# Dummy products in the first stage and a regrouped start of the output projection, in a one-core hybrid SSD / Gated DeltaNet layer

## The chip, the cores and the metric

The kernel runs on one core of one Trainium2 chip. The metric is device time in microseconds, the median of the runs shown. TensorE (PE) runs the matrix products and loads its weights on a side path (PEld); VectorE (DVE), ScalarE (ACT) and GpSimd (POOL) work beside it, and SyncE (SP) issues nearly all DMA transfers of this kernel.

## What is computed

One layer of a hybrid decoder for two request groups, 1024 prompt tokens and 64 sample tokens (8 requests of 8 tokens), 1088 in all, with the same weights. Cut to what matters:

```python
h = _rms_norm(x, norm_mix_pre) * (1 + sc1) + sh1        # sc1, sh1: from silu(c) @ w_ada + b_ada
proj = h @ w_in                                         # 1024 -> z, xbc, dt, qkv, gate, beta, alpha
...
y = _rms_norm(y_ssd * silu(z), ssd_norm_w)              # 1024 columns, chunked SSD scan
o = _rms_norm(o_gdn, gdn_norm_w) * silu(gate)           # 1024 columns, chunked Gated DeltaNet
mixed = jnp.concatenate([y, o], axis=-1)                # 2048 columns
m = mixed @ w_out
x = x + g1 * _rms_norm(m, norm_mix_post)
h = _rms_norm(x, norm_ffn_pre) * (1 + sc2) + sh2
gu = h @ w_gate_up
x = x + g2 * _rms_norm((silu(gu[..., :D_FF]) * gu[..., D_FF:]) @ w_down, norm_ffn_post)
```

The new states of both mixers, for prompt and samples, are returned too.

## The kernel before

Every float32 product is done as three matmuls of split operands: `hh` by `wh`, `hl` by `wh` and `hh` by `wl`, where `wh` is the rounded value of a weight (a cast on ACT, line 173) and `wl` the rest (a subtraction on DVE, line 174). A half of a weight tile, 128 x 512, is loaded by SP into a buffer `wr` (line 181) of a pool; the pools have few such buffers, so the next load waits until a `wr` has been split.

**Tokens** lie in three groups `TH` of 384, 384 and 320 columns; the last holds the 64 samples. There are KD = 8 blocks of 128 input columns.

**First stage.** The conditioning vector goes through `w_ada`; then the tokens are normalised (`norm_x`), turned by PE (`turned`, line 339, three transposes for a block of a group), and modulated (`modulated`, lines 357 to 368: ACT writes `hh`, DVE writes `ht` and, with POOL, `hl`; the samples' columns are added on lines 363, 365 and 367). As soon as a block is there, `first_k` (lines 416 to 418) multiplies it with the first two tiles of `w_in`: six matmuls for one block. For group 0 this is written out; for groups 1 and 2 `first_group` goes over k, modulating block k and multiplying block k-2. In between the tasks that `tick()` advances put small transposes of convolution states (`halos`, line 391). After this stage jobs take the rest of `w_in` (lines 198 to 200).

**Output projection.** `gemm_rows` is called once for each group, with 16 steps of 128 of the 2048 columns of `mixed`. A step takes a block of `mixed` (loaded by `mixed_load`, line 1331, from `mixdr`), splits it into `sh` (ACT, line 1398) and `sl` (DVE, line 1399), and multiplies with two halves of `w_out`: 18 matmuls (lines 1386, 1388, 1389) of 512 columns. Below, step 0 to step 47 counts over all three groups. In every group the steps take the DeltaNet half of the columns first (k = 8 to 15) and then the SSD half (k = 0 to 7), whose blocks are multiplied on DVE with row factors `RB` (line 1458). Weights of even k go through pool `wp`, which is shared with the work before, those of odd k through pool `wo`, which is new. The mixed blocks of groups 0 and 1 go through pool `mxp` for even k and `g_` for odd k, where `g_` takes memory that the SSD part has left; four blocks are asked for ahead. Group 2's are asked for after all tasks have ended (`settle()`), two ahead.

Beside the steps run tasks that advance with `tick()`, four times in a step: the samples' DeltaNet (`gdn_samples`, lines 1463 to 1620, with loads of `smx`, `s_d`, `s_eg` on lines 1465 to 1475), and the evacuation of a finished group.

**Order.** PE executes in the order of the program. The other engines and SP's queue are put in order by a scheduler that keeps each waiting for its operands in that order, so a load that stands behind another on SP waits for it.

Of the kernel before, what the change touches and what calls it, by code (L numbers as in the profile page):

```python
# [16 lines left out]
P = 128  # L17
# [26 lines left out]
def hybrid_step(ctx: ExitStack, tc: tile.TileContext, x_p, x_s, c_p, c_s, st_ssd, st_ssdc, st_gdn, st_gdnc,  # L44
# [100 lines left out]
    def wait(n):  # L145
        for _ in range(n):
            yield
# [109 lines left out]
    def norm_x(i):  # L257
        n = P if i < NC else NS
        xt = xts[i]
        jk = init.tile([P, D], BF16, name="jk")  # L260
        act.activation(out=jk[0:n], in_=xt[0:n], func=AF.Square, accum_out=ss[0:n, i:i + 1])
        rsqrt_small(rs[0:n, i:i + 1], ss[0:n, i:i + 1], 1.0 / D, EPS)
        dve.tensor_scalar(out=xt[0:n], in0=xt[0:n], scalar1=rs[0:n, i:i + 1], scalar2=None, op0=ALU.mult)
# [69 lines left out]
    def turned(g, k):  # L333

        n = TH[g][1]
        ps = bank()
        for w in range(0, n, P):
            r = min(P, n - w)
            pe.transpose(ps[:, w:w + r], xts[3 * g + w // P][0:r, k * P:(k + 1) * P], ident[0:r, 0:r])
        return ps  # L340
# [31 lines left out]
    def mod(g, k, ps):  # L372
        c0, n = TH[g]
        modulated(ps, k, c0, n, hh[k][:, c0:c0 + n], hl[k][:, c0:c0 + n], init, pool if k % 2 else dve)
# [34 lines left out]
    first, loads = zip(*(tile_halves(c) for c in (C_K, C_Q)))  # L409
    first_ps = [ps_a.tile([P, 512], F32, name="ps")[:, 0:TH[0][1]] for _ in first]  # L410

    def first_k(g, k, pss):
        t0, n = TH[g]
        xh, xl = hh[k][:, t0:t0 + n], hl[k][:, t0:t0 + n]
        for (hi, lo), o in zip(first, pss):
            pe.matmul(o, lhsT=hi[k], rhs=xh, start=(k == 0), stop=False)
            pe.matmul(o, lhsT=hi[k], rhs=xl, start=False, stop=False)
            pe.matmul(o, lhsT=lo[k], rhs=xh, start=False, stop=(k == KD - 1))

    def first_group(g):  # L420

        pss = [ps_a.tile([P, 512], F32, name="ps")[:, 0:TH[g][1]] for _ in first]
        for k in range(KD + 2):
            if k < KD:
                mod(g, k, turned(g, k))
            if k >= 2:
                first_k(g, k - 2, pss)
                tick()
        hid_box[g] = clock[0]
        return pss  # L430
# [36 lines left out]
    with tc.high_priority(-80):  # L467
        for i in range(3, NT):
            norm_x(i)
    for k in range(4, KD):  # L470
        first_k(0, k, first_ps)
    hid_box[0] = clock[0]
# [853 lines left out]
    mxp = ph_b.enter_context(tc.tile_pool(name="mxp", bufs=1, side="right", reuse_waits="tile"))  # L1326
    ahead = []

    def mixed_load(k, c0, n):
        t = (g_ if queue and k % 2 else mxp).tile([P, 384], F32, name="mx", bufs=3)  # L1330
        sp.dma_start(out=t[:, 0:n], in_=mixdr[k * P:(k + 1) * P, c0:c0 + n])
        return t

    settle(ssd_run)
    ph_a.close()

# [7 lines left out]
    GS = [mid.tile([NS, D], F32, name="gs0")]  # L1344
    RB = [mid.tile([P, T], F32, name=f"RB{g}") for g in range(2)]
    late_box = {}
    KS = list(range(KD, 2 * KD)) + list(range(KD))

    queue, last = [(k, *TH[gi]) for gi in range(2) for k in KS], []
    for i in range(4):  # L1350
        ahead.append(mixed_load(*queue.pop(0)))

    def load_gains(i, gp, gs):
        sp.dma_start(out=gp, in_=gaindr[i][0].partition_broadcast(P))
# [95 lines left out]
    def mixed_piece(c0, n):  # L1450
        def piece(k):
            m = ahead.pop(0)
            if queue or last:
                ahead.append(mixed_load(*(queue or last).pop(0)))
            if k < KD:
                while "RB" not in late_box:
                    tick()
                dve.scalar_tensor_tensor(out=m[:, 0:n], in0=m[:, 0:n], scalar=W_SSDN[:, k:k + 1],
                                         in1=RB[k // 4][:, c0:c0 + n], op0=ALU.mult, op1=ALU.mult)
            return m[:, 0:n]  # L1460
        return piece

    def gdn_samples():
        smx = g_.tile([P, HG, 4, NS], F32, name="smx")
        sp.dma_start(out=smx, in_=smdr)
        smp, smv, smg = smx[:, :, 0:2, :], smx[:, :, 2, :], smx[:, :, 3, :]
        ko = g_.tile([NS, HG, P], F32, name="s_ko")
# [5 lines left out]
        sp.dma_start(out=d0, in_=accr[16:24, NP:T].partition_broadcast(NS))  # L1473
        eg = g_.tile([P, HG, NS], F32, name="s_eg")
        sp.dma_start(out=eg, in_=eaccr[16:24, NP:T].partition_broadcast(P))
        yield from wait(16)
        for a in range(2):
            ps = bank()
            pv = ps.rearrange("p (h n) -> p h n", n=P)
# [227 lines left out]
    def second_half():  # L1707
# [5 lines left out]
        yield from wait(8)  # L1713
        yield from flips(GRP[1][1:], t, 2 * HN, 6 * P)

    def w_out_half(k, hf):
        return load_half(w_out[k * P:(k + 1) * P, hf * 512:hf * 512 + 512], wp=wo if k % 2 else wp)

    ph_f = ExitStack()
    for gi, grp in enumerate(GRP):  # L1720
# [19 lines left out]
            xts[i] = hv  # L1740
            return after

        gemm_rows(grp, KS, w_out_half, mixed_piece(c0, n), mid, done)
        if gi == 1:
            settle()
            last += [(k, *TH[2]) for k in KS]
            for i in range(2):
                ahead.append(mixed_load(*last.pop(0)))
            ph_s.close()
            ph_c.close()  # L1750
            acs_ = ctx.enter_context(tc.tile_pool(name="acs", bufs=2, reuse_waits="tile"))
            wf = ctx.enter_context(tc.tile_pool(name="wf", bufs=1, reuse_waits="tile"))
            h2b = ph_f.enter_context(tc.tile_pool(name="h2b", bufs=1, reuse_waits="tile"))
            blocks(h2b, 0)
            x1t = xts
            spawn(later(second_half(), 22))
        elif gi == 0:
            spawn(later(flips(GRP[0], xts, 0, 3 * P), FLIP))
# [214 lines left out]
```

## Time and profile before

| what | value |
|---|---|
| median of 3 runs | 2013.7 us |
| lowest and highest run | 2012.06 and 2014.39 us |
| the profiled execution | 2012.82 us |
| its span in the trace | 2011.0 us |
| PE, busy share of the span | 97% |
| DVE, ACT, POOL busy shares | 67%, 51%, 6% |
| mean granted clock of PE | 0.987 |

A page of the profile gives, for one execution, the busy time of each engine and the chain of work that ended last. Views of the trace answer narrower questions: a table of waits says what an engine sat idle for; a timeline gives single instructions with the idle time before them in brackets and who ended it; a table of windows gives busy time of every engine in a stretch with the granted clock of PE, where 1.00 is 2.4 GHz and 0.50 is 1.2 GHz. Times in a timeline are us from the start of the span. The first 87 us are the first stage; the output projection runs from about 1003 to 1266 us.

### The profile page before, as it was taken

How to read it: one execution, taken by the hardware profiler on the slowest of the kernel's cores; microseconds unless marked ns; L12 is line 12 of the kernel's file. 1: busy time of each engine (PE TensorE's matmuls, PEld its weight loads, DVE VectorE, ACT ScalarE, POOL GpSimd, SP SyncE). 2: the span in 40 equal slices, each digit the busy share in tenths (PEclk: the TensorE clock that was granted, in tenths of full speed). 3: DMA queues.
4: the chain of work that ended last, by engine and by line, in shares of the span. 5: the costliest groups of instructions: out<-in, count | busy, mean ns of one | idle time of the engine just before them, and what ended most of it. 6: DMA issues, size and time to landing. Idle time of an engine off the chain costs nothing.

```text
span 2011.0 us, 35475 instructions
## 1 busy us (share of the span) xinstructions
PE 1951.5 (97%) x13211; PEld 1753.8 (87%) x13211; DVE 1351.1 (67%) x2964; ACT 1035.2 (51%) x2578; POOL 125.9 (6%) x184
## 2 busy tenths in 40 slices
PE   6999999999999999999969999999999999999998
PEld 4898899999999998998857677899999999988886
DVE  4669767877887766867657767885555556645465
ACT  4455455554655446777435666753333334544454
POOL 2100000000000001100011010100000000000000
PEclk9799999999999999999989999999999999999999
DMA  8223323322211127555267855422222224633131
GB/s 300 56 60 102 97 81 110 100 81 87 84 52 55 59 83 189 177 138 159 77 212 228 258 184 192 127 75 81 75 76 82 76 81 128 225 125 110 46 100 50
DMA packets 223142, 235.29 MB, mean 117 GB/s; under 512 B 19018, under 2 KB 177252, under 8 KB 222842
## 3 DMA queue, kind: packets, MB, share of 16 engines
q1 hardware_dynamic: 220266, 228.86, 36.8%
q10 hardware_dynamic: 2384, 3.05, 0.4%
q8 instruction: 104, 1.70, 0.3%
q0 software_dynamic: 320, 1.12, 0.2%
q14 instruction: 68, 0.56, 0.1%
HBM read 188.83 MB, written 44.15 MB: 116 GB/s over the span
## 4 chain that ended last, share of the span: by engine, by line
PE 84%; DVE 6%; ACT 3%; DMA 3%; issue 2%; SPq 1%; POOL 1%; DVEq 0%; POOLq 0%; ACTq 0%
PE ps L198 9%; PE ps L199 8%; PE ps L200 8%; PE ps L1874 7%; PE ps L1873 7%; PE ps L1875 7%; PE ps L1386 7%; PE ps L1389 7%; PE ps L1388 6%; PE ps L741 2%; PE ps L795 1%; DMA wr<-in_w_out_dram 1%; PE ps L704 1%; DVE uc L891 1%; DMA L<-accr 1%
## 5 line engine op out<-in xcount | busy, mean ns | idle before, releaser
L198 PE MATMUL ps<-hh,wh 128*128 128x384 f32 (+1 forms) x1200 | 425.6, 355 | 0.1
L200 PE MATMUL ps<-hh,wl 128*128 128x384 f32 (+1 forms) x1200 | 393.0, 327 | 0.0
L199 PE MATMUL ps<-hl,wh 128*128 128x384 f32 (+1 forms) x1200 | 392.6, 327 | 0.0
L1386 PE MATMUL ps<-wh,sh 128*128 128x512 f32 x678 | 274.6, 405 | 16.0 <-ACT wh L173 15.2
L1389 PE MATMUL ps<-wl,sh 128*128 128x512 f32 x678 | 267.7, 395 | 0.2 <-DVE wl L174 0.2
L198 PEld LDWEIGHTS ps<-hh,wh 128*128 128x128 f32 x1200 | 227.1, 189 | 17.1 <-issue 11.5
L1388 PE MATMUL ps<-wh,sl 128*128 128x512 f32 x604 | 237.6, 393 | 3.7 <-DVE sl L1399 3.7
L199 PEld LDWEIGHTS ps<-hl,wh 128*128 128x128 f32 x1200 | 227.3, 189 | 0.8
L200 PEld LDWEIGHTS ps<-hh,wl 128*128 128x128 f32 x1200 | 226.0, 188 | 0.0
L173 ACT CAST wh<-wr 128x512 fp32r<-128x512 f32 x200 | 122.7, 621 | 171.0 <-PE ps L199 84.5
L174 DVE TENSOR_TENSOR wl<-wr,wh 128x512 fp32r<-128x512 f32 x200 | 136.8, 691 | 58.5 <-ACT wh L173 57.8
L1386 PEld LDWEIGHTS ps<-wh,sh 128*128 128x128 f32 x678 | 128.4, 189 | 52.4 <-ACT wh L173 15.6
L174 DVE TENSOR_TENSOR wl<-wd,wh 128x512 fp32r<-128x512 f32 x130 | 89.6, 692 | 118.1 <-ACT wh L173 114.8
L1389 PEld LDWEIGHTS ps<-wl,sh 128*128 128x128 f32 x678 | 128.4, 189 | 30.3 <-DVE wl L174 0.8
L173 ACT CAST wh<-wd 128x512 fp32r<-128x512 f32 x130 | 80.7, 621 | 139.0 <-PE ps L1388 100.3
L1388 PEld LDWEIGHTS ps<-wh,sl 128*128 128x128 f32 x604 | 114.5, 190 | 27.3 <-DVE sl L1399 4.5
L1810 ACT CAST wh<-s 128x512 fp32r<-128x512 f32 x104 | 64.4, 620 | 83.1 <-PE ps L1874 74.6
L1873 PE MATMUL ps<-T_0h,wh 128*128 128x272 f32 x352 | 102.0, 290 | 3.3 <-DVE u L1889 1.8
L1874 PE MATMUL ps<-T_0l,wh 128*128 128x272 f32 x352 | 101.6, 289 | 0.0
L1874 PE MATMUL ps<-T_1l,wh 128*128 128x272 f32 x352 | 101.6, 289 | 0.0
L1875 PE MATMUL ps<-T_0h,wl 128*128 128x272 f32 x352 | 101.3, 288 | 0.0
L1875 PE MATMUL ps<-T_1h,wl 128*128 128x272 f32 x352 | 101.3, 288 | 0.0
(496 smaller groups left out, 4442.6 us busy)
## 6 DMA issues: line engine op xcount, KB each, us to landing
wr<-in_w_in_dram SPq DMA_DIRECT2D x104, 256.0 KB
wr<-in_w_gate_up_dram SPq DMA_DIRECT2D x104, 256.0 KB
wr<-in_w_out_dram SPq DMA_DIRECT2D x96, 256.0 KB
w<-in_w_ada_dram SPq DMA_DIRECT2D x16, 1024.0 KB
wd<-in_w_down_dram SPq DMA_DIRECT2D x22, 512.0 KB
actdr<-as SPq DMA_DIRECT2D x18, 544.0 KB
L<-accr SPq DMA_DIRECT2D x16, 544.0 KB
am<-actdr SPq DMA_DIRECT2D x44, 192.0 KB
```

What stands on the lines that cost most here:

```text
L173: act.copy(wh, src)
L174: low.tensor_tensor(out=wl, in0=src, in1=wh.bitcast(F32), op=ALU.subtract)
L198: pe.matmul(out, lhsT=hi[k], rhs=xh[k], start=(k == 0), stop=False)
L199: pe.matmul(out, lhsT=hi[k], rhs=xl[k], start=False, stop=False)
L200: pe.matmul(out, lhsT=lo[k], rhs=xh[k], start=False, stop=(k == KD - 1))
L1386: pe.matmul(o, lhsT=sh[:, cs], rhs=wh, start=first, stop=False)
L1388: pe.matmul(o, lhsT=sl[:, cs], rhs=wh, start=False, stop=False)
L1389: pe.matmul(o, lhsT=sh[:, cs], rhs=wl, start=False, stop=last)
L1810: act.copy(wh, opa[p])
L1873: pe.matmul(o, lhsT=wh[:, cs], rhs=bh[:, m, :], start=(m == 0 and not on), stop=False, **on)
L1874: pe.matmul(o, lhsT=wh[:, cs], rhs=bl[:, m, :], start=False, stop=False, **on)
L1875: pe.matmul(o, lhsT=wl[:, cs], rhs=bh[:, m, :], start=False, stop=(m == 3), **on)
```

## The change

It has three parts. First, a function `keep_busy(n)` issues n products of the first modulated block with the first weight block into a bank of PSUM that nobody reads: 14 before group 0's blocks 4 to 7, and 10 each before `first_k(1, 0)` and `first_k(2, 0)`. Second, in the output projection the pools of the weights go by the number of the step: steps 0 and 1 use `wp`, then even steps `wo` and odd steps `wp`. Mixed blocks: the first three in `mxp`, then odd ones of groups 0 and 1 in `g_`, all of group 2 in `mxp`; three are asked for ahead instead of four (two from group 2 on), in one queue over all groups, and group 2 takes its steps in the order k = 0 to 15. Third, `gdn_samples` issues its loads 6 ticks later and everything after them 4 ticks, which is one step, later.

```diff
+    def keep_busy(n):
+
+        ps = bank()
+        for i in range(n):
+            pe.matmul(ps[:, 0:384], lhsT=first[0][0][0], rhs=hh[0][:, 0:384], start=True, stop=True)
+
...
         for k in range(KD + 2):
             if k < KD:
                 mod(g, k, turned(g, k))
+            if k == 2:
+                keep_busy(10)
             if k >= 2:
...
     with tc.high_priority(-80):
         for i in range(3, NT):
             norm_x(i)
+    keep_busy(14)
     for k in range(4, KD):
         first_k(0, k, first_ps)
...
-    def mixed_load(k, c0, n):
-        t = (g_ if queue and k % 2 else mxp).tile([P, 384], F32, name="mx", bufs=3)
-        sp.dma_start(out=t[:, 0:n], in_=mixdr[k * P:(k + 1) * P, c0:c0 + n])
-        return t
...
-    KS = list(range(KD, 2 * KD)) + list(range(KD))
-
-    queue, last = [(k, *TH[gi]) for gi in range(2) for k in KS], []
-    for i in range(4):
-        ahead.append(mixed_load(*queue.pop(0)))
+
+    KS = [list(range(KD, 2 * KD)) + list(range(KD))] * 2 + [list(range(2 * KD))]
+    queue = [(gi, k) for gi in range(3) for k in KS[gi]]
+    asked = [0]
+
+    def mixed_load():
+
+        i = asked[0]
+        asked[0] += 1
+        gi, k = queue[i]
+        c0, n = TH[gi]
+        t = (g_ if gi < 2 and i > 2 and i % 2 else mxp).tile([P, 384], F32, name="mx", bufs=3)
+        sp.dma_start(out=t[:, 0:n], in_=mixdr[k * P:(k + 1) * P, c0:c0 + n])
+        ahead.append(t)
+
+    for i in range(3):
+        mixed_load()
...
             m = ahead.pop(0)
-            if queue or last:
-                ahead.append(mixed_load(*(queue or last).pop(0)))
+            while asked[0] < len(queue) and len(ahead) < (3 if asked[0] < 4 * KD else 2):
+                mixed_load()
...
     def gdn_samples():
         smx = g_.tile([P, HG, 4, NS], F32, name="smx")
+        yield from wait(6)
         sp.dma_start(out=smx, in_=smdr)
...
-        yield from wait(16)
+        yield from wait(14)
...
+    steps = [0]
+
     def w_out_half(k, hf):
-        return load_half(w_out[k * P:(k + 1) * P, hf * 512:hf * 512 + 512], wp=wo if k % 2 else wp)
+        steps[0] += 1
+        return load_half(w_out[k * P:(k + 1) * P, hf * 512:hf * 512 + 512],
+                         wp=wo if steps[0] > 4 and steps[0] % 4 in (1, 2) else wp)
...
-        gemm_rows(grp, KS, w_out_half, mixed_piece(c0, n), mid, done)
+        gemm_rows(grp, KS[gi], w_out_half, mixed_piece(c0, n), mid, done)
         if gi == 1:
             settle()
-            last += [(k, *TH[2]) for k in KS]
-            for i in range(2):
-                ahead.append(mixed_load(*last.pop(0)))
             ph_s.close()
```

In the changed program `first_k` has lines 422 to 424, the dummy products line 416, the output projection's matmuls lines 1402, 1404 and 1405, `mixed_load` line 1363 and the samples' loads lines 1482 to 1492.

The first place is PE at the start of group 2 of the first stage: the last transposes of the first three blocks (`w` holds normalised tokens), then the products of block 0. Before:

```order
154 L339 MATMUL ps<-ident,w_389 128x128
155 L339 MATMUL ps<-ident,w_391 128x64
156 L416 MATMUL ps<-hh_133,wh 128x320
157 L417 MATMUL ps<-hl_141,wh 128x320
158 L418 MATMUL ps<-hh_133,wl 128x320
```

And now:

```order
156 L339 MATMUL ps<-ident,w_389 128x128
157 L339 MATMUL ps<-ident,w_391 128x64
158 L416 MATMUL ps<-hh_133,wh 128x384 x10
159 L422 MATMUL ps<-hh_133,wh 128x320
160 L423 MATMUL ps<-hl_141,wh 128x320
161 L424 MATMUL ps<-hh_133,wl 128x320
```

Ten products that need only old operands stand between the transposes and the products that wait for the new `hh` and `hl`.

The second place is SP's queue at the start of the output projection (`y` is the last SSD block on its way to `mixdr`; `wr` rows are halves of `w_out`, `mx` rows mixed blocks). Before, the two `wr` of row 307 are those of step 8, the two of row 313 those of step 1, the first that go through pool `wo`:

```order
306 L1253 DMA mixdr<-y 128x1088
307 L181 DMA wr<-in_w_out_dram 128x512 x2
308 L1331 DMA mx<-mixdr 128x384 x2
309 L1465 DMA smx<-smdr 128x2048
310 L1473 DMA s_d_11581<-accr 64x8x64
311 L1475 DMA s_eg<-eaccr 128x8x64
312 L1331 DMA mx<-mixdr 128x384
313 L181 DMA wr<-in_w_out_dram 128x512 x2
314 L1331 DMA mx<-mixdr 128x384
```

And now, where the two `wr` of row 309 are those of step 7, and the two of row 315 those of step 2:

```order
307 L1262 DMA mixdr<-y 128x1088
308 L1363 DMA mx<-mixdr 128x384
309 L181 DMA wr<-in_w_out_dram 128x512 x2
310 L1363 DMA mx<-mixdr 128x384
311 L1482 DMA smx<-smdr 128x2048
312 L1490 DMA s_d_11675<-accr 64x8x64
313 L1492 DMA s_eg<-eaccr 128x8x64
314 L1363 DMA mx<-mixdr 128x384
315 L181 DMA wr<-in_w_out_dram 128x512 x2
316 L1363 DMA mx<-mixdr 128x384
```

The samples' loads keep their place directly ahead of the first halves that go through `wo`; those halves now belong to step 2 instead of step 1.

The third place is DVE in the same stretch. Before, the two first of the three `wl` of row 1648 are those of step 1:

```order
1640 L1252 TENSOR_TENSOR y<-y,sz 128x1088
1641 L174 TENSOR_TENSOR wl<-wr,wh 128x512
1642 L1258 TENSOR_TENSOR sqs<-sqs,sz 128x1088
1643 L174 TENSOR_TENSOR wl<-wr,wh 128x512
1644 L1399 TENSOR_TENSOR sl<-mx,sh 128x384 x3
1645 L1489 TENSOR_TENSOR s_d_11581<-s_d_11581,rate_510 64x512
1646 L1491 TENSOR_SCALAR s_d_11581<-s_d_11581 64x512
1647 L1493 TENSOR_TENSOR s_d_11581<-s_d_11581,tri_106 64x512
1648 L174 TENSOR_TENSOR wl<-wr,wh 128x512 x3
```

And now, where the two `wl` of row 1653 are those of step 2:

```order
1641 L1261 TENSOR_TENSOR y<-y,sz 128x1088
1642 L1415 TENSOR_TENSOR sl<-mx,sh 128x384
1643 L174 TENSOR_TENSOR wl<-wr,wh 128x512 x2
1644 L1267 TENSOR_TENSOR sqs<-sqs,sz 128x1088
1645 L174 TENSOR_TENSOR wl<-wr,wh 128x512
1646 L123 TENSOR_SCALAR rsg<-ps 128x8
1647 L123 TENSOR_SCALAR rsg<-ps 64x1
1648 L174 TENSOR_TENSOR wl<-wr,wh 128x512
1649 L1415 TENSOR_TENSOR sl<-mx,sh 128x384 x2
1650 L1506 TENSOR_TENSOR s_d_11675<-s_d_11675,rate_525 64x512
1651 L1508 TENSOR_SCALAR s_d_11675<-s_d_11675 64x512
1652 L1510 TENSOR_TENSOR s_d_11675<-s_d_11675,tri_106 64x512
1653 L174 TENSOR_TENSOR wl<-wr,wh 128x512 x2
```

The `sl` of steps 1 and 2 moved ahead, one to row 1642 and one to just above row 1641. The `wl` of step 1 left this stretch, it stands before the last SSD block now; the samples' rows L1506 to L1510 still stand ahead of the first `wl` that goes through `wo`.

## Rows read from the trace of the kernel before

**Rows 1.** The page: chain that ended last, shares of the span by engine.

```profile
PE 84%; DVE 6%; ACT 3%; DMA 3%; issue 2%; SPq 1%; POOL 1%; DVEq 0%; POOLq 0%; ACTq 0%
```

**Rows 2.** Table of what PE waited for, whole span: us, times, longest.

```profile
PE ps L1386 <- ACT wh L173: 15.2, 1, 15.2
...
PE ps L1388 <- DVE sl L1399: 3.7, 1, 3.7
...
PE ps L417 <- DVE hl L368: 3.2, 3, 1.6
...
PE ps L1873 <- ACT as L1880: 1.1, 2, 0.7
```

**Rows 3.** Windows: us, busy PE, PEld, DVE, ACT, POOL, granted clock, DMA share, GB/s.

```profile
54.00:61.00 7.00, 6.88 (x46) 6.48 (x43) 4.40 (x9) 2.69 (x4) 3.11 (x3) 1.00 0.01 2
66.70:84.57 17.87, 17.87 (x79) 14.20 (x78) 8.51 (x29) 4.86 (x12) 2.69 (x3) 0.52 0.12 30
70.00:80.00 10.00, 10.00 (x49) 7.51 (x47) 4.62 (x16) 2.65 (x6) 0.87 (x1) 0.50 0.03 5
87.00:1003.00 916.00, 906.46 (x6706) 842.16 (x6706) 681.13 (x1698) 515.22 (x1463) 65.30 (x89) 1.00 0.34 99
1003.00:1033.00 30.00, 14.80 (x61) 11.40 (x58) 13.48 (x22) 8.60 (x14) 2.59 (x2) 0.72 0.75 239
1033.00:1198.00 165.00, 162.97 (x932) 117.32 (x931) 113.93 (x221) 96.41 (x242) 18.88 (x26) 1.00 0.71 219
```

**Rows 4.** PE timeline, groups 0 and 1: start, us, instruction, idle before it.

```profile
39.52 0.44 PE L417 MATMUL ps<-hl,wh 128*128 128x384 f32 x1 [1.37 <-DVE hl L368]
...
40.33 0.52 PE L417 MATMUL ps<-hl,wh 128*128 128x384 f32 x1
40.65 0.52 PE L418 MATMUL ps<-hh,wl 128*128 128x384 f32 x1
...
43.79 0.33 PE L417 MATMUL ps<-hl,wh 128*128 128x384 f32 x1
43.96 0.33 PE L418 MATMUL ps<-hh,wl 128*128 128x384 f32 x1
...
46.69 0.33 PE L339 MATMUL ps<-ident,w 128*128 128x128 f32 x1 [1.13 <-DVE rs L123]
```

**Rows 5.** PE timeline, group 2 and the first job after it.

```profile
62.60 1.79 PE L339 MATMUL ps<-ident,w 128*128 128x128 f32 x9
...
66.25 0.41 PE L417 MATMUL ps<-hl,wh 128*128 128x320 f32 x1 [0.30 <-DVE hl L368]
...
70.52 1.04 PE L391 MATMUL ps<-ident,w 24*128 24x24 f32 x8
...
87.06 0.45 PE L198 MATMUL ps<-hh,wh 128*128 128x384 f32 x1
```

**Rows 6.** SP timeline, start of the output projection: start and us of each issue.

```profile
1011.92 0.42 SPq L1465 DMA_DIRECT2D smx<-smdr  x1
...
1015.64 1.07 SPq L181 DMA_DIRECT2D wr<-in_w_out_dram  x2
```

**Rows 7.** ACT timeline there, the casts of step 1.

```profile
1022.40 1.28 ACT L173 CAST wh<-wr 128x512 fp32r<-128x512 f32 x2 [0.27 <-DMA wr<-in_w_out_dram]
```

**Rows 8.** PE timeline, steps 1 and 2 of the output projection.

```profile
1023.07 0.79 PE L1386 MATMUL ps<-wh,sh 128*128 128x512 f32 x1 [15.20 <-ACT wh L173]
...
1026.22 0.47 PE L1388 MATMUL ps<-wh,sl 128*128 128x512 f32 x1
...
1031.87 0.63 PE L1386 MATMUL ps<-wh,sh 128*128 128x512 f32 x1
```

**Rows 9.** DVE timeline ahead of the pause in group 2, step 10.

```profile
1232.05 0.55 DVE L1458 SCALAR_TENSOR_TENSOR mx<-mx,prm1T,RB 128x320 f32<-128x320 f32 x1
```

**Rows 10.** The chain of waits in 1105 to 1145 us: start, us, what.

```profile
1133.43 4.85 DMA mx<-mixdr
```

**Rows 11.** ACT timeline, first casts of the gate and up weights.

```profile
1261.43 0.62 ACT L1810 CAST wh<-s 128x512 fp32r<-128x512 f32 x1 [3.04 <-PE ps L1386]
```

## Prediction

> **What bounds the kernel now.** I read the chain first: PE has 84% of it, DVE 6%, transfers 3% [rows 1]. So a microsecond counts where PE pauses or runs at its lower clock, and nearly nowhere else. The table of PE's waits gives the pauses [rows 2]: one of 15.2 us for a cast of weights (line 1386), one of 3.7 us for an `sl` (line 1388), three for `hl` in the first stage, 3.2 us together. The windows give the clock [rows 3]. Look at 70 to 80 us: PE is busy 10.0 of 10.0 us and the granted clock is 0.50, the 1.2 GHz level. A table of waits shows nothing there, yet half the speed is lost. From 54 to 61 us the same loop, with group 1, had 1.00. In 87 to 1003 us PE is busy 906.46 of 916 at clock 1.00: what arrives earlier at 87 us arrives earlier at 1003. From 1003 to 1033 us PE is busy only 14.80 of 30 us at 0.72: that is the start of the output projection. From 1033 to 1198 us it is again busy 162.97 of 165.
>
> **The 34 products, group 0 and group 1.** They cost PE 0.17 us each at full clock (starts 43.79 and 43.96) and 0.32 at the low one (40.33 and 40.65) [rows 4]: 5.8 us in all, and they are free only in a pause. The 14 (2.4 us) stand in front of block 4, where PE waits for `hl` until 39.52. With the clock kept up, the ten matmuls behind it would save 10 x 0.15 = 1.5 us. But the next transposes wait at 46.69 for `rs`, normalised tokens that DVE and POOL make without PE [rows 4]; PE only gets there earlier and waits longer. Gain 0. The 10 of group 1 come right after. That longer pause may itself lower the clock, and then the ten take 3.2 instead of 1.7 us, 1.5 us more; the pause that they stand in is one of the three of 3.2 us together, about half of that [rows 2], so some 1.2 us of loss is the worse end. If the clock stays up, some ten matmuls are spared 0.15 us each, and the arithmetic for later blocks stops part of that: 1.0 at best. I take +0.3, nearer the middle, since both levels are likely there.
>
> **The 10 of group 2.** The nine transposes from 62.60 end at 64.4; the first product that waits for `hl` starts at 66.25 [rows 5]. Ten products of 0.17 us are 1.7 and fill that pause without making anyone late. After this pause the clock went down and stayed down to 84 us although PE never paused: in 66.70 to 84.57 us it is busy 17.87 of 17.87 at a mean of 0.52 [rows 3]. At full clock the same PE work takes 17.87 x 0.52 = 9.3 us, 8.6 less. Next in line is DVE: 8.51 us busy in that stretch [rows 3], just under 9.3, and the chain from transposes through `hh`, `ht` and `hl` back to PE cannot overlap perfectly; two subtractions of weights also stand ahead of an `hl`. I charge 1.8 us for these. Gain 8.6 - 1.8 = 6.8. Ends: 8.6, and 1.0 if the clock falls again after one step or less.
>
> The Trainium skill, "TensorE: Matmul & The Clock Gate", in Part 4 on the transposes of PE, says that the full clock does not engage for transposes, because they do not count as busy in the same way. That speaks against this part, since each step of group 2 holds eleven. By that rule alone the gain would be near the lower end. The row of 54 to 61 us [rows 3] differs with it in so far as three transposes in each step went with a clock of 1.00 there.
>
> **The start of the output projection.** PE does step 0, pauses 15.2 us, and starts step 1 at 1023.07 [rows 2, 8], when ACT has cast the two halves of `w_out` (1022.40, after waiting for their transfer) [rows 7]. These are the first that go through pool `wo`. On SP they stand behind the samples' loads (1011.92) and a mixed block, and are issued at 1015.64 [rows 6]. The change does not turn this round: by the order of SP the samples' loads still stand directly ahead of the first halves in `wo`. But these now belong to step 2. Step 1 has its weights from `wp`, loaded and split with those of step 0, and its mixed block early, so it runs inside what was a pause, as does the sum of squares behind it (line 1265 before). So PE resumes with step 2 at about the time at which it resumed with step 1, where before step 2 began at 1031.87: 1031.87 - 1023.07 = 8.8 us [rows 8]. From this comes off what the low clock takes anew. After the pause seven matmuls took 3.15 us (1023.07 to 1026.22) at half speed, 1.5 too much; that loss is in the 8.8 and comes again, less the 0.6 that the first three of step 2 lose before too. 8.8 - 0.9 = 7.9. And the restart may be up to 1.1 us later: an `sl` (0.55 us by the like-sized row of line 1458 [rows 9]) moved ahead of the last `y`, whose transfer the mixed blocks wait for, and one more issue stands on SP. I take 0.9 of it, since both lie straight on the path. Gain 7.0, ends 5 and 8.
>
> **The rest of the edits.** The pause of 3.7 us in group 2 [rows 2] stands behind a block of arithmetic for the gate and up weights on DVE. The block stays, by the order; only one multiply by `RB` of 0.55 us [rows 9], which group 2 now does in its first eight steps instead of its last eight, goes from in front of it. Gain 0.5, ends 0 and 2. Those eight multiplies, 4.4 us, now meet the evacuation of group 1; they have as much time per step as the others, and I book nothing, with a loss of up to 1.5 in the range. The last step of group 2 takes its weights through `wp`, so the first casts of the gate and up weights, at 1261.43 [rows 11], must wait for its end, some 5 us later; PE's wait for line 1880 there is 1.1 us now [rows 2], and I add 0.5, ends 0 and 1.5. The samples' arithmetic one step later moves work on DVE and POOL against the steps, with small waits on either side: 0, ends -2 and +2.
>
> **Sum.** 0 + 0.3 + 6.8 + 7.0 + 0.5 - 0.5 = 14.1 us. The profiled execution took 2012.8 us, with 1.8 us outside its span of 2011.0; from it the sum gives 1998.7. It lies 0.9 us under the median of the runs, 2013.7, from which I forecast **1999.6 us**.
>
> **Rivals.** *The clock falls again in group 2* (1). For it: a step there has eight small transposes beside the three, as the low stretch had, and PE was busy without pause there and yet stayed at 0.50 [rows 3]. Against it: the level only went down after a pause, and the same loop with three transposes ran at 1.00. Then that term is 0 to 1: 14.1 - 6.8 + 0.5, so 7.8 us gained, 2005.9. *The wait moves with the weights* (2): if the memory of `wo` or the transfers ahead of it (DMA is 0.75 busy in 1003 to 1033 us [rows 3]) make step 2's halves land a step later than step 1's did, the 7.0 goes to about 0: 2006.6. This is also the case in which the start does not do what the change says. Against it: the halves are issued behind the same loads as before. *The lead of the mixed blocks is too short* (3), the slower side: with three ahead instead of four (two in group 2), a load that sits behind a blocked weight load on SP lands after ACT wants it. For it: already now a load of 4.85 us, from 1133.43, lies in the chain [rows 10]. Against it: the scheduler put the loads at about the same places between the weights. It would act in steps 16 to 47, 32 of them; at 14.1 / 32 = 0.44 us a step it eats all, and at the 1 us by which such a load might well be late, PE loses 32: 2013.7 - 14.1 + 32 = 2031.6. *Both gains stay away* (4): rivals 1 and 2 together, 2013.
>
> **How the numbers follow.** The forecast has 0.64, rival 1 0.14, rival 2 0.09, rival 4 0.05, and rival 3 0.08, of which 0.03 with so small a price that it comes out near the old time. The forecast's own ends are about 1996 and 2004; rivals 1 and 2 add 2004 to 2008. The range of 1996.0 to 2008.5 holds most of these three. A change of 0.2%, 4.0 us, is about what a measurement of this kernel can tell from none. Faster: 0.64 + 0.14 + 0.09, less 0.02 for their tails, 0.85. Same: 0.05 + 0.03 + 0.02 = 0.10. Slower: 0.05.
>
> **What would show it.** In the changed kernel's trace: a granted clock near 1.00 in the 12 us after the ten products of group 2, and the first job (line 198) starting near 80 instead of 87.06 [rows 5]; the pause of group 0's end unchanged or longer. At the output projection 36 matmuls before the pause instead of 18, the pause about 10 us instead of 15.2, and still ended by a cast of weights. After it, no new waits of PE for `sh` or `sl` in steps 16 to 47. The prediction is wrong if the clock reads 0.50 behind the products, if the pause stays at 15 us, or if PE's busy share between the two places falls.

## The result

The changed kernel took 1998.55 us by the median of four runs, against 2014.05 us before. One of the four, of 3822.06 us, was disturbed: the median of the other three is 1997.33 us, and their ratio to before is 0.9916, 95% interval [0.9895, 0.9937]. The forecast was 1999.6 us, range 1996.0 to 2008.5. The profiled execution took 1993.87 us with a span of 1991.8 us, 19.2 us less than the 2011.0 before. Later rounds gave 1994.55 against 2014.03 and 1993.93 against 2015.72, a little below that range. The 13 other runs of the changed kernel, over all rounds, lie between 1990.6 and 1999.8 us; this spread is a finding of its own, below.

I followed the same matmul through both traces. The table gives how much earlier than before PE reaches it (start before minus start after, us from each span's start).

| place in PE's program | before | after | earlier by |
|---|---|---|---|
| transposes ahead of group 2, first stage | 62.60 | 61.63 | 1.0 |
| first job (line 198) | 87.06 | 80.50 | 6.6 |
| output projection, step 0 | 1003.46 | 995.09 | 8.4 |
| step 3 | 1036.73 | 1020.02 | 16.7 |
| step 31 (last of group 1) | 1193.83 | 1179.94 | 13.9 |
| step 42 | 1237.76 | 1223.90 | 13.9 |
| step 43 | 1246.77 | 1227.55 | 19.2 |
| step 47 (last of group 2) | 1263.29 | 1244.03 | 19.3 |
| first product with w_down | 1740.20 | 1721.24 | 19.0 |

What PE waited for, whole span, after (us in total, times, longest); compare [rows 2]:

```profile
PE ps L1402 <- ACT wh L173: 6.3, 1, 6.3
...
PE ps L1608 <- DVE s_ut L1599: 2.4, 1, 2.4
PE ps L339 <- DVE rs L123: 2.2, 2, 1.1
...
PE ps L1671 <- DVE s_S L1620: 1.4, 1, 1.4
...
PE ps L423 <- DVE hl L368: 1.0, 3, 0.4
```

The 15.2 us for the first halves in `wo` are 6.3 (line 1402, before 1386), the 3.7 us for an `sl` have left the table, and two waits on the samples' arithmetic are new (lines 1608 and 1671).

Windows after (us, busy PE, PEld, DVE, ACT, POOL, granted clock, DMA share, GB/s), against [rows 3]:

```profile
48.00:62.00 14.00, 13.68 (x85) 12.04 (x84) 10.70 (x20) 7.54 (x13) 5.65 (x6) 1.00 0.33 78
62.00:80.00 18.00, 16.74 (x108) 13.33 (x108) 13.14 (x41) 7.51 (x20) 4.17 (x7) 1.00 0.16 39
80.00:995.00 915.00, 906.91 (x6709) 842.25 (x6707) 684.58 (x1701) 516.19 (x1465) 65.99 (x89) 1.00 0.34 100
995.00:1030.00 35.00, 28.62 (x121) 22.53 (x120) 17.75 (x31) 12.32 (x23) 3.99 (x5) 0.85 0.80 253
1030.00:1190.00 160.00, 155.19 (x896) 110.98 (x895) 116.07 (x227) 97.69 (x246) 21.19 (x27) 1.00 0.70 216
```

Group 2 of the first stage is at clock 1.00 throughout. At the start of the output projection PE is busy 28.62 of 35 us, where it was 14.80 of 30. From 1030 to 1190 us it now idles 4.8 us, where 2.0 were lost in the like stretch before.

PE's timeline of group 2, after (start, us, instruction, idle before it and who ended it):

```profile
61.63 1.79 PE L339 MATMUL ps<-ident,w 128*128 128x128 f32 x9
63.35 2.01 PE L416 MATMUL ps<-hh,wh 128*128 128x384 f32 x10
...
65.35 0.35 PE L423 MATMUL ps<-hl,wh 128*128 128x320 f32 x1
...
68.21 0.67 PE L391 MATMUL ps<-ident,w 24*128 24x24 f32 x8
68.81 0.64 PE L339 MATMUL ps<-ident,w 128*128 128x128 f32 x3
...
70.46 0.67 PE L391 MATMUL ps<-ident,w 24*128 24x24 f32 x8
...
74.68 0.41 PE L423 MATMUL ps<-hl,wh 128*128 128x320 f32 x1 [0.38 <-DVE hl L368]
...
80.50 0.44 PE L198 MATMUL ps<-hh,wh 128*128 128x384 f32 x1
```

The ten products fill the pause: the first product that needs `hl` follows without a wait (65.35), where it waited before [rows 5]. A step takes 2.25 us (68.21 to 70.46) instead of 3.79 before, from 70.52 [rows 5] to

```profile
74.31 1.04 PE L391 MATMUL ps<-ident,w 24*128 24x24 f32 x8
```

The Trainium skill, "TensorE: Matmul & The Clock Gate", Part 4, says that the full clock does not engage for PE's transposes. Before, steps with transposes among their matmuls stayed at the low level for nearly all of 17.87 us of busy PE [rows 3], as that sentence would have it; now the same steps, entered at the full level, kept it over 18 us. Three of them have eleven transposes ahead of their six matmuls, one has seven and the others have nine, three or none (the prediction gave all of them eleven). So the Trainium skill and this trace differ, and the trace decides for this kernel; whether transposes alone would bring the clock up no run here shows.

The start of the output projection, PE and then SP, after:

```profile
1001.85 0.40 PE L1405 MATMUL ps<-wl,sh 128*128 128x512 f32 x1
1002.34 2.15 PE L1274 MATMUL ps<-ones,sqs 128*128 128x1 f32 x18
...
1013.64 0.80 PE L1402 MATMUL ps<-wh,sh 128*128 128x512 f32 x1 [6.29 <-ACT wh L173]
```

```profile
1002.23 0.42 SPq L1482 DMA_DIRECT2D smx<-smdr  x1
...
1006.89 1.21 SPq L181 DMA_DIRECT2D wr<-in_w_out_dram  x2
```

Step 1 and the sums of squares run before the pause, the last six matmuls of step 1 at the low level (0.43 us from one start to the next instead of 0.23). The halves of step 2 are issued 11.8 us after step 0 began (995.09 to 1006.89), those of step 1 were issued 12.2 us after (1003.46 to 1015.64 [rows 6]): the wait has kept its cause and its place on SP, and PE does one step more ahead of it.

### The profile page after: what moved, and what is told of

The parts are those of the page before. It is cut to its first block, busy times and chain, and to the rows that moved or that the text cites. A ratio compares the mean times of both kernels' runs of the same rounds, so it can differ in the third digit from the quotient of the medians.

```text
span 1991.8 us, 35533 instructions
## 1 busy us (share of the span) xinstructions
PE 1946.4 (98%) x13245; PEld 1750.1 (88%) x13245; DVE 1353.9 (68%) x2964; ACT 1035.8 (52%) x2578; POOL 127.6 (6%) x184
## 4 chain that ended last, share of the span: by engine, by line
PE 83%; DVE 7%; ACT 4%; DMA 2%; issue 2%; POOL 1%; SPq 1%; DVEq 0%; POOLq 0%; ACTq 0%
PE ps L198 9%; PE ps L199 8%; PE ps L200 8%; PE ps L1892 7%; PE ps L1891 7%; PE ps L1893 7%; PE ps L1402 7%; PE ps L1405 7%; PE ps L1404 6%; PE ps L750 2%; PE ps L804 1%; DVE tm L906 1%; DVE rr L908 1%; DVE uc L900 1%; PE ps L1201 1%
## 5 line engine op out<-in xcount | busy, mean ns | idle before, releaser
L174 DVE TENSOR_TENSOR wl<-wr,wh 128x512 fp32r<-128x512 f32 x200 | 136.0, 690 | 55.7 <-ACT wh L173 55.2
L1829 DVE TENSOR_TENSOR wl<-wr,wh 128x512 fp32r<-128x512 f32 x78 | 53.8, 691 | 70.2 <-ACT wh L1828 68.9
```

The lines of the kernel that those rows point to most:

```text
L174: low.tensor_tensor(out=wl, in0=src, in1=wh.bitcast(F32), op=ALU.subtract)
```

## The experiments

Each was timed beside the kernel before on the same chip; "before" names the median in those rounds.

### One part alone

**Only the 34 products**, put into the kernel before; nothing else changed.

```diff
+    keep_busy(14)
     for k in range(4, KD):
...
+            if k == 2:
+                keep_busy(10)
```

> The kernel before with the 34 products alone; the output projection is that of before. Theory (the gains are separate): PE starts the output projection 8.4 us earlier, as in the trace of the changed kernel, and nothing behind it takes this back: about 2005.7 us against 2014.1, with the pause of 15.2 us and the pause of 3.7 us in group 2 unchanged. Rival (the clock falls anyway in most executions, as transposes do not hold it): 2011 to 2013 us, granted clock near 0.5 behind the products of group 2. Rival (an early start meets transfers that are not earlier): the pause of 15.2 grows by up to 8 us and the time stays near 2014.

2005.16 us against 2014.03, ratio 0.9955 [0.9941, 0.9969]: 8.9 us, as expected by the median. Step by step it is another sum: its profiled execution, the fastest of the six (1999.43 us), is 5.9 us earlier than before at the first job, 11.7 at step 0 and 14.5 at step 43. Its table of waits keeps the 15.2 us nearly whole, and 2.5 of the 3.7, which the theory had unchanged:

```profile
PE ps L1395 <- ACT wh L173: 15.0, 1, 15.0
...
PE ps L1397 <- DVE sl L1408: 2.5, 1, 2.5
```

**Only the output projection**, the changed kernel without products.

```diff
-    keep_busy(14)
...
-            if k == 2:
-                keep_busy(10)
```

> The changed kernel without the 34 products. Theory (the gains are separate): the first stage is that of before (87 us to the first job), the output projection keeps its gain of 8.4 us at step 3, loses about 4 us beside the samples' arithmetic up to step 31 and gains 5.4 us back at step 42, where a late mixed block held up DVE before: about 2003.5 us. Rival (the pause at step 42 went because of another phase between the transfers and PE that the products brought): it comes back, and the time is 2008 to 2009 us.

2003.46 us against 2014.03, ratio 0.9947 [0.9935, 0.9959]: 10.6 us. Relative to before, PE is 0.0 us earlier at step 0, 8.3 at step 3, 4.9 at step 31 and 10.1 at step 43. This is the ledger of the full change less its first stage, and 8.9 + 10.6 = 19.5 us is what the full change gained in those rounds. By the medians the two parts add up, though each is known to 2 or 3 us only. In the traces they are not quite independent: between steps 42 and 43 the products alone gain 2.5 us, this part alone 5.4 and both together 5.4. The pause at step 42 is gone here too, so the products were not needed to remove it.

### Which products count

**Only the ten of group 2.**

```diff
-    keep_busy(14)
...
-            if k == 2:
+            if k == 2 and g == 2:
                 keep_busy(10)
```

> The changed kernel with only the ten products of group 2; the 14 of group 0 and the ten of group 1 are left out. Theory (group 0's gain is eaten by the wait for normalised tokens, and group 1's is about nothing): the first job starts within 0.5 us of the changed kernel's 80.5 to 81.3, and the median is the same within 1.5 us, 1994 to 1997. Rival (the clock of groups 0 and 1 counts, or their products keep the clock up for group 2): first job at 82 to 87 us, 1998 us or more.

1997.12 us against 2012.61, ratio 0.9925 [0.9906, 0.9944]. The first job starts at 82.61, 0.5 to 2.1 us later than in the ten profiled executions with the 34 products and no more (80.50 to 82.09). That is in the range of the rival, while the median lies between the two theories. Group 2 itself takes the same: 18.85 us from its transposes (63.76) to the first job, 18.87 in the changed kernel, 24.46 before. So the ten products of group 2 bring 5.6 us whatever the others do. What the 24 others bring is less clear. With them group 2 begins at 61.6 to 61.9 us in the three executions in which the clock of group 1 stays up, and at 62.3 to 63.2 in the seven in which it falls all the same. Without them it begins at 63.76 here, but at 62.60 before and at 62.66 in the run with the output projection alone, whose programs do the same up to that point. One trace is too few to price them. The window of this one reads

```profile
48.00:62.00 14.00, 12.29 (x61) 11.38 (x60) 9.56 (x19) 6.79 (x12) 6.04 (x6) 0.76 0.30 78
```

**15 products more in group 2**, three in each of the steps 3 to 7.

```diff
             if k == 2:
                 keep_busy(10)
+            elif k > 2 and k < KD and g == 2:
+                keep_busy(3)
```

> The changed kernel with three more products in each of the steps k = 3 to 7 of group 2 in the first stage, 15 in all, 2.6 us of PE at full clock. The undisturbed runs of the changed kernel fall in two sets, 1991.4 to 1994.6 us with a mean clock of 0.995 or 0.996, and 1997.3 to 1999.8 us with 0.990 to 0.992. Theory (in the second set the clock falls in group 2 in spite of the ten products): with more products there the second set is rarer or gone, every run has 0.994 or more, and the median is 1993 to 1996 us, the first job 0.5 to 2.5 us later. Rival (the second set loses its clock elsewhere, after the first stage): both sets stay, and every run is 1 to 2.5 us slower.

1999.06 us against 2012.61, ratio 0.9945 [0.9923, 0.9967]. Group 2 takes 20.60 us (61.51 to 82.11), 1.7 more than with ten products: of 2.6 us of products, the steps' own waits hide 0.9. The spread stays, 1996.1 to 2005.9 us, with mean clocks from 0.989 to 0.995, as the rival said. The theory on the second set of runs falls; a profiled execution with a mean clock of 0.991 (the samples at ticks 16 and 24, below) also has its 18.86 us for group 2.

### The samples

**The samples' work at its old ticks.**

```diff
-        yield from wait(6)
         sp.dma_start(out=smx, in_=smdr)
...
-        yield from wait(14)
+        yield from wait(16)
```

> The changed kernel with the samples' loads and arithmetic at the ticks of before (0 and 16 instead of 6 and 14 after). Theory (the delay by a step is what costs 3.8 us between steps 16 and 31, as the samples' arithmetic then meets the evacuation of group 0): 1.5 to 4 us faster than the changed kernel, with the pause of 2.4 us at the samples' second product gone. Rival (the delay protects the start): the loads keep their place on SP, but the samples' first arithmetic stands ahead of the casts of step 2, and the restart at step 2 is later by as much; no change or slower, up to 4 us.

1994.75 us against 2014.03, ratio 0.9914 [0.9901, 0.9927]; the changed kernel in the same rounds had 1994.55. No change, but not for the rival's reason: step 3 comes at the same time. Relative to before, this version falls from 16.8 us earlier to 15.0 at step 5, where PE waits for the samples' first arithmetic (line 1520 in it), and from 14.9 to 13.4 at steps 32 and 33, behind the evacuation of group 1:

```profile
PE ps L1520 <- DVE s_ko L1501: 1.8, 1, 1.8
```

The delayed one falls from 16.7 to 13.9 between steps 9 and 31, with the waits of 2.4 and 1.4 us shown above. Two places, one price of about 3 us. I take it that PE, which gets 8 us ahead at the start, uses up slack that the samples' work had, and that their ticks only decide where it shows; this is argued from the two traces and not shown by a run of its own.

**The samples' loads behind step 2's weights** (ticks 10 and 20 instead of 6 and 20).

```diff
-        yield from wait(6)
+        yield from wait(10)
         sp.dma_start(out=smx, in_=smdr)
...
-        yield from wait(14)
+        yield from wait(10)
```

> The changed kernel with the samples' loads 10 ticks after the start instead of 6 (their arithmetic stays at tick 20): by the order of SP they now stand behind the two halves of step 2 instead of ahead of them. Theory (the 1.4 MB of samples' loads ahead on SP set the restart at step 2): the halves land some 4 us earlier, the pause of 6.3 to 6.8 us becomes 2 to 3 us, and step 3 starts some 4 us earlier; a later wait of the samples' arithmetic may take part of it back, 1991 to 1994 us by the median. Rival (the memory of the new pool or the last y's transfer sets it): the pause stays at 6 to 7 us and so does the time, 1994 to 1998.

2002.13 us against 2012.61, ratio 0.9951 [0.9931, 0.997]: by the ratios slower than the changed kernel in its three rounds (0.9916, 0.9906 and 0.9893), although its first effect is what the theory said. SP, PE and DVE of this version:

```profile
1004.35 0.90 SPq L181 DMA_DIRECT2D wr<-in_w_out_dram  x2
1005.29 0.43 SPq L1482 DMA_DIRECT2D smx<-smdr  x1
```

```profile
1009.81 0.80 PE L1402 MATMUL ps<-wh,sh 128*128 128x512 f32 x1 [1.63 <-ACT wh L173]
1026.34 0.80 PE L1405 MATMUL ps<-wl,sh 128*128 128x512 f32 x1 [5.51 <-DVE wl L174]
```

```profile
1024.47 0.62 DVE L1474 SCALAR_TENSOR_TENSOR mx<-mx,prm1T,RB 128x384 f32<-128x384 f32 x1 [7.10 <-DMA RB<-rsdr]
1025.00 0.68 DVE L1510 TENSOR_TENSOR s_d<-s_d,tri 64x512 f32<-64x512 f32 x1
1025.61 1.88 DVE L174 TENSOR_TENSOR wl<-wr,wh 128x512 fp32r<-128x512 f32 x3
```

The pause fell from 6.3 to 1.6 us, so the samples' loads ahead on SP did set it. But in the order that followed, the first multiply by the row factors `RB` stood on DVE ahead of the splits of step 4. It waited 7.10 us for the factors, and the weights behind it with it: PE stood 5.5 us, and behind that pause its clock was at the low level.

**The samples' loads behind step 4's weights** (ticks 16 and 20). Its order on DVE has that multiply behind the splits of step 4.

```diff
-        yield from wait(6)
+        yield from wait(16)
...
-        yield from wait(14)
+        yield from wait(4)
```

> The changed kernel with the samples' loads 16 ticks after the start (their arithmetic stays at tick 20). By the order of SP they now stand behind the halves of steps 2 and 4; on DVE the first multiply by the row factors now stands behind the splits of step 4, where in the kernel with the loads at 10 ticks it stood ahead of them and waited 7.1 us for its factors. Theory (that multiply, not the transfers themselves, took the 5.6 us back): step 3 starts 5 us earlier after step 0 than in the changed kernel, and step 7 still 3 to 5 us earlier; a pause for the samples' data may come in steps 5 to 8, as they land later; 1991 to 1994 us. Rival (the transfers of this stretch are the bound, whatever their order): step 8 starts no earlier than in the changed kernel, and the time is 1995 to 2000 us.

1992.3 us against 2012.78, ratio 0.9899 [0.9884, 0.9913]. Step 3 starts 19.5 us after step 0 (changed kernel: 24.9), step 8 46.9 us (51.4).

```profile
1007.12 0.80 PE L1402 MATMUL ps<-wh,sh 128*128 128x512 f32 x1 [2.10 <-ACT wh L173]
```

```profile
1020.29 0.62 DVE L1474 SCALAR_TENSOR_TENSOR mx<-mx,prm1T,RB 128x384 f32<-128x384 f32 x1 [6.16 <-DMA RB<-rsdr]
```

DVE still waits 6.16 us for the factors, and PE does not notice, since nothing that it needs stands behind. The transfers were not the bound; the order of two queues was.

**The same with the samples' arithmetic a step later** (ticks 16 and 24; `wait(8)` instead of `wait(4)`).

> As the kernel with the samples' loads at 16 ticks, with their arithmetic at tick 24, one step later than in the changed kernel. Theory (the samples' data are late at tick 20 and hold up DVE): step 8 starts 3 to 5 us earlier than in the changed kernel, without a pause in steps 5 to 8, and steps 16 to 31 lose 0 to 3 us more than it; 1991 to 1995 us. Rival (the transfers are the bound): as the other kernel, 1995 to 2000 us.

1995.75 us against 2012.78, ratio 0.992 [0.9904, 0.9936]: no better than the changed kernel. Step 8 starts 53.3 us after step 0, 1.9 later than in the changed kernel, where the theory had 3 to 5 earlier. In its profiled execution, the slowest of the six runs, a second pause of 3.5 us for a cast of weights stands ahead of step 6; why that cast came late I have not followed. With the arithmetic at tick 20 PE had waited 0.8 us for the samples' data, so the later tick had little to gain.

**Both once more, in the same rounds.**

> The kernel with the samples' loads at 16 ticks once more, beside the changed kernel on the same chip. In one profiled execution of each it started step 8 of the output projection 4.4 us earlier after step 0 than the changed kernel, and step 32 4.2 us earlier. Theory (that gain is kept to the end): median 3 to 5 us under the changed kernel's in the same rounds, 1991 to 1993 us. Rival (it is taken back by the clock in other stages, or its first times were a good draw): less than 2 us apart.

> The changed kernel once more, for that comparison: 1994 to 1998 us by the median, its runs between 1991 and 2000. The spread goes with the mean clock: those above 1997 us have 0.992 or less, those below 1995 us have 0.994 or more.

1989.66 us, ratio 0.9878 [0.9857, 0.9898], beside 1993.93 us, ratio 0.9893 [0.9874, 0.9911], against 2015.72 before. The medians are 4.3 us apart. In the traces of these rounds too, step 8 starts 4.8 us earlier after step 0 than in the changed kernel, and step 32 4.3 us. The intervals overlap, so the times alone do not prove the difference. Of what I expected of the changed kernel's spread one run fell just outside: 1997.53 us with a mean clock of 0.993.

### The pause at step 42

**Group 2 in the old order of steps**, all else as changed.

```diff
-    KS = [list(range(KD, 2 * KD)) + list(range(KD))] * 2 + [list(range(2 * KD))]
+    KS = [list(range(KD, 2 * KD)) + list(range(KD))] * 3
```

> The changed kernel with group 2 of the output projection in the old order of steps (k = 8 to 15, then 0 to 7), with the new queue of mixed blocks. Before, a row factor multiply (line 1458) waited 3.5 us on DVE for a mixed block in step 41, which pushed the sums for the gate weights ahead of the sl of step 42. Theory A (the order of steps removed it: the multiplies stand in the last eight steps again, and there a late block holds up DVE): the pause before step 42 is back with 2.5 to 4 us, and with the lower clock behind it 4 to 6 us are lost: 1999 to 2002 us. Theory B (the queue of mixed blocks removed it: the block is there in time in either order): no pause, and the time is within 1 us of the changed kernel, 1994 to 1997.

1998.59 us against 2012.61, ratio 0.9935 [0.9913, 0.9957]. A pause of 1.6 us in step 42 is back, and 1.9 us are lost there against the changed kernel; the clock did not fall behind it (1.00 from 1220 to 1228 us). The row that I had not followed in the trace of before stands on DVE at 1226.30 us, and it is here too, at 1207.50; first before, then this version:

```profile
1226.30 0.55 DVE L1458 SCALAR_TENSOR_TENSOR mx<-mx,prm1T,RB 128x320 f32<-128x320 f32 x1 [3.49 <-DMA mx<-mixdr]
```

```profile
1207.50 0.55 DVE L1474 SCALAR_TENSOR_TENSOR mx<-mx,prm1T,RB 128x320 f32<-128x320 f32 x1 [3.82 <-DMA mx<-mixdr]
```

A multiply by the row factors waits for a late mixed block and holds up the sums for the gate weights, and these hold up the `sl` of step 42. In the new order the multiplies are done by step 40, and no such wait is left; DVE waits there for a cast of weights instead (2.6 us in the changed kernel, at 1207.40), and PE does not notice. Theory A has the mechanism; its size was 1.9 us and not 4 to 6. All profiled executions agree: in the three with the old order the multiply waits 3.5 to 3.9 us and the pause is there, 3.7 us before, 2.5 with products alone, 1.6 here; in the eleven with the new order the `sl` starts 0.90 us ahead of the step, although PE reaches it at times 15 us apart. What makes the pause differ among the three is not settled.

### The spread

**The changed kernel once more.**

> The changed kernel once more, since its three undisturbed runs lie between 1993.9 and 1999.8 us, wider than those of before. Theory (spread by the clock): an execution near 1998 to 2000 us shows a stretch at granted clock 0.5 that the first trace (1993.9 us, mean clock 0.995) does not have, in the first stage or behind the pause of the output projection, and the mean clock is 0.990 or 0.991. Rival (spread by transfers): the mean clock is the same 0.995 and the extra time lies in waits for mixed blocks or weights in steps 2 to 31. Median 1996 to 1999.5.

1994.55 us against 2014.03, ratio 0.9906 [0.9891, 0.992]. Runs of 1991.4, 1991.8 and 1994.6 us had mean clocks of 0.995, 0.995 and 0.996, those of 1998.1 and 1998.3 had 0.991 and 0.992. The time goes with the clock. Its profiled execution, 1991.4 us, shows what the low level does to group 1:

```profile
46.66 0.48 PE L339 MATMUL ps<-ident,w 128*128 128x128 f32 x1 [1.15 <-DVE rs L123]
...
48.06 2.87 PE L416 MATMUL ps<-hh,wh 128*128 128x384 f32 x10
```

Here the ten products took 2.87 us, in the first execution of the changed kernel 1.99, and the first job came at 81.26 instead of 80.50. None of the slower runs of the changed kernel was profiled, so what was expected of their traces could not be tested. One profiled execution of a sister kernel had the lower clock, that with ticks 16 and 24 (2002.8 us, 0.991). Windows of it, and of the first execution of the changed kernel:

```profile
228.00:232.00 4.00, 3.60 (x43) 3.44 (x44) 3.16 (x5) 1.84 (x7) 1.76 (x1) 0.82 0.18 53
232.00:236.00 4.00, 4.00 (x54) 3.50 (x54) 1.97 (x3) 0.00 (x0) 0.84 (x1) 0.50 0.00 0
236.00:240.00 4.00, 4.00 (x14) 4.00 (x13) 1.79 (x3) 0.00 (x0) 0.10 (x1) 0.50 0.01 4
```

```profile
228.00:232.00 4.00, 4.00 (x44) 3.43 (x43) 2.47 (x5) 1.26 (x5) 2.61 (x1) 0.69 0.06 16
232.00:236.00 4.00, 4.00 (x62) 3.96 (x62) 3.22 (x5) 0.00 (x0) 0.00 (x0) 0.88 0.00 0
236.00:240.00 4.00, 4.00 (x37) 2.89 (x36) 2.01 (x4) 2.02 (x3) 0.10 (x1) 1.00 0.19 22
```

Among jobs and small products of the DeltaNet part the clock fell in both, and in the sister kernel it stayed low; PE lost 3.0 us there against the other, far from everything that the change touches. In the same place the second profile of the changed kernel stays at 1.00. So one stage outside the change falls in some executions and not in others. That this alone makes the second set is not shown, since its other runs have no trace.

## Why the prediction was right, and where it was not

The sum of 14.1 us was near the 15.5 of the first medians (2014.05 less 1998.55) and under the 19.2 of the profiled execution and the 19.5 and 21.8 of later rounds. The two large terms had the right mechanism. That the sum came near is in part luck: three other terms were outside their ranges or missing, and their errors partly cancel. By its steps:

- **Group 0**, 0 forecast. This was right. The products kept the clock, the matmuls behind them ended 1.4 us earlier, and PE then waited for `rs` twice, 2.2 us in place of 1.1.
- **Group 1**, +0.3 (-1.2 to 1.0). It was 0.7 to 1.0 in the three of the ten executions in which the clock stayed up, and -0.6 to 0.3 in the seven in which it fell. The range named both.
- **Group 2**, +6.8 (1.0 to 8.6). It was 5.6 in all eleven executions with ten products there. The mis-sized term is "the same PE work takes 17.87 x 0.52": transposes do not go with the clock as matmuls do. Eight small ones took 1.04 us at the low level [rows 5] and 0.67 at the full one, so a step fell to 2.25 us and not to 3.79 x 0.52 = 1.97. The waits for `hl`, for which 1.8 us were charged, came to 1.3 us, 0.38 at 74.68 and these two:

```profile
77.73 0.42 PE L423 MATMUL ps<-hl,wh 128*128 128x320 f32 x1 [0.42 <-DVE hl L368]
79.35 0.42 PE L423 MATMUL ps<-hl,wh 128*128 128x320 f32 x1 [0.47 <-POOL hl L368]
```

  Rival 1 did not occur in any profile. But the reason given against it, that the level only went down after a pause, was misread: before, it also went down at 101.36 us, behind small products and with no pause of PE ahead of it.

```profile
98.25 2.19 PE L537 MATMUL ps<-fold,smc 64*128 64x32 f32 x18
...
101.97 0.52 PE L199 MATMUL ps<-hl,wh 128*128 128x384 f32 x1
```

- **The start of the output projection**, +7.0 (5 to 8). It was 8.3, just outside. The term of the restart was wrong in sign: I charged 0.9 us for a later restart, and it came 1.1 us earlier after step 0 (18.55 us instead of 19.61). Of that 0.4 us lie ahead of the issue of the halves and 0.7 behind it; what made them earlier is not followed. The price of the lower clock was 1.5 us (step 2 to step 3 took 6.38 instead of 4.86), where I had taken 0.9 net. The pause was 6.3 us and not about 10 (15.2 less some 6.2 for step 1 and the sums of squares at the full clock, plus 0.9): 2.0 of the difference are the restart (1.1 earlier instead of 0.9 later), and most of the rest is the low clock of step 1's last six matmuls, which now run before the pause and for which I had no term.
- **The samples' delay**, 0 (-2 to 2). It was -2.8, outside. I had asked what the delay does, but the run at the old ticks loses as much in another place; that PE comes earlier is the likely cause.
- **The pause in group 2**, +0.5 (0 to 2). It was 5.4: the pause of 3.7 us and the lower clock behind it, all gone. I took the block of sums for the cause because it stood in front, and did not ask why it stood there so late. The wait of 3.49 us on DVE was to be read in the trace of before.
- **The start of the gate and up products**, -0.5 (-1.5 to 0). It was -0.8, which is in the range.
- **Not in the sum**: what happens between the first job and step 0, which the prediction took to pass on any gain unchanged. There PE gains another 1.8 us in the first profiled execution, and from -1.5 to 5.8 us in the other eleven with products. Three places make most of it. Before, the clock fell for some matmuls from 101 to 105 us (1.6 us), and did not in nine of the twelve. Near 238 and 880 us it falls in some executions and not in others. And the trace of before has a wait at 788 us that the run with the output projection alone, which has no products, does not have either; all twelve gain 2.3 to 2.9 us there, that run 1.7:

```profile
788.17 1.38 PE L1202 MATMUL ps<-cT,hS 128*128 128x128 f32 x6 [1.68 <-DVE hS L1181]
```

  So part of the 19.2 us may be the draw of the one profiled execution of before, and not the change.

Rival 3, the short lead of the mixed blocks, did not come: no new wait of PE for `sh` or `sl` from step 16 to 47. Rival 2 failed with the pause of 6.3 us.

## What to carry to other kernels

In this kernel a pause of PE could cost more than its own length, by what the lower clock took behind it. Where such a pause cannot be removed, products that nobody reads are worth trying: ten of them, 1.9 us of PE in a pause that was there anyway, brought 5.6 us in group 2. They do not always help: the ten of group 1 kept the clock up in three of ten executions, the gain of the 14 of group 0 went into the next wait, and 15 more in group 2 only cost 1.7 us. When a wait is moved and not removed, ask what stands in the same queue behind its new place; from step 0 to step 32 the same loads cost 7.1 us behind step 2 and gained 4.2 behind step 4. And when a block of work seems to cause a pause, find out why the block was late before putting a price on the pause.

## What was not expected of the hardware

The low level can hold for long while PE is busy without a break: 10.0 of 10.0 us at 0.50 before [rows 3], and 4.0 of 4.0 us twice in the windows above. In both cases many small products or transposes stood among the matmuls; that they held it there is not shown. The clock also fell without a pause ahead of it, behind 18 products of 32 columns before (98.25 us) and behind 18 of one column now (1002.34 us). Summed over windows of 4 us, as (1 - granted clock) x 2 x 4 us, the low level lasted 53 us before and 21 us in the changed kernel's first profile. PE was busy for some 40 and 14 us of that, and idle for the rest, in the pauses of the output projection and at the end. That leaves a difference of 26 us of work, and at half speed up to 13 of the 19 us gained. And the same kernel spreads over 9 us from run to run, with its mean clock.
